# A gated delta rule on raw keys and queries: norms as factors by token and in the output norm's eps

## The chip, the cores and the metric

One core of one Trainium2 chip runs the kernel. The metric is the device time of one launch in microseconds (us), the median of three runs; the kernel before takes 2573.53 us (2573.46 to 2574.1). The engines are TensorE (PE, its weight loads PEld), VectorE (DVE), ScalarE (ACT), GpSimd (POOL) and SyncE (SP), which issues most DMAs.

## The reference, cut to what matters

The reference is a decoder trunk of two layers on 256 tokens of width 2048: a mixer, a cross attention and a convolutional feed-forward net in each layer, all in float32. The change is in the mixer of layer 0, which joins eight stick-breaking attention heads with eight gated delta rule heads of 128 features. For each delta head:

```python
def l2norm(x):
    return x * lax.rsqrt(jnp.sum(x * x, axis=-1, keepdims=True) + EPS)

gq, gk, gv = split(silu(causal_dwconv(gdn_qkv, sconv_w)))
o_b = gated_delta_rule(l2norm(gq), l2norm(gk), gv, log_decay, beta)
o_b = rmsnorm(o_b, gdn_norm) * silu(gdn_gate)
# in gated_delta_rule, by chunks of 64 tokens, q scaled by dk ** -0.5:
neg_n = -where(tri_strict, (k * beta) @ k.T * decay, 0)
t_inv = (1 - neg_n) ** -1                     # by doubling
u = t_inv @ (v * beta);  w = t_inv @ (k * beta * exp(gc))
attn = q @ k.T * decay;  q_g = q * exp(gc);  k_dec = k * exp(gc_last - gc)
# per chunk: v_new = u - w @ state; o = q_g @ state + attn @ v_new
#            state = state * exp(gc_last) + k_dec.T @ v_new
```

So keys and queries each get a norm per token before the rule, and the rule's output gets an RMS norm per token, with EPS = 1e-6 in all of them.

## The kernel before, in words

Activations lie with features on the 128 partitions and the 256 tokens along the free axis. Weights stream from HBM through SP's queue in slabs of 128 x 1024 (`raw`, five buffers). ACT casts each to a high part (`hi`, L250), DVE computes the rest (`lo`, two instructions of 512 columns, L259), and `mm_tile` multiplies them: per step of 128 input features a 512-column matmul on `hi` (L287) and a 256-column one on `lo` (L288). After each such step it calls `side.tick()`.

`Side` holds side chains, written as Python generators. A tick runs at most one step of one chain that is due; `yield n` asks for n ticks until the next step. So the stream of projections on TensorE carries the small work of the heads between its matmuls, in program order as the compiler's scheduler then places it. Three chains at most are open (four from the stick heads on).

The mixer of layer 0 is `even()`. Its order: the first projection while the input arrives; `decays` (from L506), a side chain that makes the per-token factors `g`, `gc`, `bt` (beta), `nbt` (minus beta), `beg` (beta times exp of the summed decay) and `ekd`; then `delta_head` for the eight delta heads, with four projections each (key, query, value, gate: 4 x 16 ticks), in pairs; after each pair a side chain `delta_pair` is spawned. Then come `values` and `stick_head` for the stick-breaking heads, whose chains (`stick_chain`) use `nsu`. The output projection reads the delta heads' results first.

`delta_pair` before, for two heads at once:

- L604 to L607: `squares_of` for the keys and for the queries of both heads: a square (L585, ACT), its float32r part (L586, ACT) and the rest (L587, POOL).
- L608 to L614: `sum_squares`, two 256-column matmuls with a matrix of ones (L593), which gives the sum over the features to every partition; `rsqrt`, a root with one correction (L353 DVE; L355, L356, L358 ACT; L359, L361 DVE) on 256 columns, with single-buffered tiles; and the scaled key or query into `kq` (L613, DVE).
- L616 to L624: `gs`, the summed decays (L621), and `pk`, the products of the keys with keys and queries (L623).
- L625 to L638: the decay factors by `Exp`, then the strict products `p0` (scaled by `nbt`), the attention `at`, and `qg`.
- L640 to L652: transposes of keys and values (L645, L646) and their scaled forms `kbe`, `kd`, `vb` on ACT.
- L655 to L711: p's transpose (L658) and the inverse by doubling (L683, L685, L691, L693); L714 to L753: `u` and `w`, and the four chunks of the state, with the output in PSUM, `po`.
- L755 to L764: the output norm, by `squares_of` and `sum_squares` and one root for each head, the gain (L760), the gate (L761) and the split into two parts (L236, L237).

The PSUM tiles of these steps come from `acc()`, a pool of three buffers. In SBUF the tags `kq0` and `kq` have two buffers each; the stick heads use both tags again.

Of the kernel before, what the change touches and what calls it, by code (L numbers as in the profile page):

```python
# [10 lines left out]
F32 = mybir.dt.float32  # L11
# [3 lines left out]
ALU = mybir.AluOpType  # L15
# [41 lines left out]
CEV = ["B64", "H0", "H1", "U64", "nSU", "nones", "maskT", "mask2", "I64", "maskS"]  # L57
# [90 lines left out]
def build(tc, nc, a):  # L148
# [303 lines left out]
    def even():  # L452
# [12 lines left out]
        for k in range(KD):  # L465
# [7 lines left out]
            if k == 2:  # L473
                wab = [e(f"wab{i}", (P, 512), 2, F32R, "kq0") for i in range(2)]
                A.copy(wab[0], early["ab", 0])
                V.tensor_tensor(out=wab[1], in0=early["ab", 0], in1=f32(wab[0]), op=ALU.subtract)
# [17 lines left out]
        cev = e("cev", (P, 3 * P), tag="sbv")  # L494
        cst = e("cst", (P, 7 * P))
        C = {k: cev[:, q * P:q * P + P] for q, k in enumerate(CEV[:3])}
        C.update({k: cst[:, q * P:q * P + P] for q, k in enumerate(CEV[3:])})
# [8 lines left out]
        def decays():  # L506
            nc.sync.dma_start(cev, a["cev"][:, 0:3 * P])
            nc.sync.dma_start(cst, a["cev"][:, 3 * P:10 * P])
# [20 lines left out]
            V.tensor_scalar(out=g, in0=sl, scalar1=-1.0, scalar2=None, op0=ALU.mult)  # L529
            sigmoid_(bt, ab[:, :, 8:16])  # L530
# [35 lines left out]
        def delta_head(h):  # L566
            kq0 = e("kq0", (P, 2, S), 2)
# [12 lines left out]
        onesr = e("onesr", (P, P), dt=F32R)  # L580

        def squares_of(x):

            sq, sp = tmp("sq", bufs=2), e("sqs", (P, 2, S), 4, F32R, "sqs")
            A.activation(sq, x, AF.Square)  # L585
            A.copy(sp[:, 0], sq)  # L586
            G.tensor_tensor(out=sp[:, 1], in0=sq, in1=f32(sp[:, 0]), op=ALU.subtract)  # L587
            return sp

        def sum_squares(sp):  # L590
            ps = acc()
            for i in range(2):
                T.matmul(ps[:, 0:256], lhsT=onesr, rhs=sp[:, i], start=i == 0, stop=i == 1)  # L593
            return ps

        def delta_pair(h0, kq0s, vs, sgts):

            cc = lambda z, t, i: z[:, t, h0 + i:h0 + i + 1]
            two = range(2)
            if h0 == 0:  # L600
                A.copy(onesr, ones)
            vec = lambda n: e(n, (P, 2, P), 2)
            kq = [e("kq", (P, 2, 2, P), 2) for _ in two]
            sps = []  # L604
            for q in range(2):
                sps.append([squares_of(kq0s[i][:, q]) for i in two])
                yield 6  # L607
            for q in range(2):  # L608
                for i in two:
                    ps = sum_squares(sps[q][i])  # L610
                    r = rsqrt(ps, 256, 1.0).rearrange("p (t n) -> p t n", t=2)
                    z = kq0s[i][:, q].rearrange("p (t n) -> p t n", t=2)
                    V.scalar_tensor_tensor(out=kq[i][:, :, q], in0=z, scalar=P ** -0.5 if q else 1.0, in1=r, op0=ALU.mult, op1=ALU.mult)  # L613
                yield 14 if q else 4  # L614
# [3 lines left out]
            for i in two:  # L618
# [3 lines left out]
                for t in range(2):  # L622
                    T.matmul(pk[:, t * 256:t * 256 + 256], lhsT=kq[i][:, t, 0], rhs=kq[i][:, t].rearrange("p q n -> p (q n)"), start=True, stop=True)  # L623
                pks.append(pk)  # L624
            p0, at, qg = ([vec(n) for _ in two] for n in ("p0", "atf", "qg"))  # L625
            for i in two:
                pk = pks[i].rearrange("p (t c) -> p t c", t=2)
# [6 lines left out]
                A.activation(qg[i].rearrange("p t n -> p (t n)"), gs[:, i * 256:i * 256 + 256], AF.Exp)  # L634
                for t in range(2):
                    V.scalar_tensor_tensor(out=p0[i][:, t], in0=pk[:, t, 0:P], scalar=cc(nbt, t, i), in1=p0[i][:, t], op0=ALU.mult, op1=ALU.mult)
                V.tensor_tensor(out=at[i], in0=pk[:, :, P:2 * P], in1=at[i], op=ALU.mult)
                G.tensor_tensor(out=qg[i], in0=kq[i][:, :, 1], in1=qg[i], op=ALU.mult)  # L638
            yield 5
            kbe, vb = ([vec(n) for _ in two] for n in ("kbe", "vb"))  # L640
            kd = [e("kd", (P, 4, P), 2) for _ in two]
            for i in two:
                px = acc()
                for t in range(2):
                    T.transpose(px[:, t * 256:t * 256 + 128], kq[i][:, t, 0], ident)  # L645
                    T.transpose(px[:, t * 256 + 128:t * 256 + 256], vs[i][:, t * P:t * P + P], ident)  # L646
                for t in range(2):
                    pt = px[:, t * 256:t * 256 + 128]
                    A.activation(kbe[i][:, t], pt, AF.Identity, scale=cc(beg, t, i))
                    for b in range(2):  # L650
                        A.activation(kd[i][:, 2 * t + b], pt, AF.Identity, scale=cc(ekd[:, b], t, i))
                    A.activation(vb[i][:, t], px[:, t * 256 + 128:t * 256 + 256], AF.Identity, scale=cc(bt, t, i))  # L652
# [102 lines left out]
            sps = [squares_of(po[:, i * 256:i * 256 + 256]) for i in two]  # L755
            yield 12
            for i in two:
                pn = sum_squares(sps[i])
                r = rsqrt(pn, 256, 1.0 / P)
                V.scalar_tensor_tensor(out=r, in0=po[:, i * 256:i * 256 + 256], scalar=col("gdn"), in1=r, op0=ALU.mult, op1=ALU.mult)  # L760
# [3 lines left out]
                mix[8 + h0 + i] = x  # L764

# [8 lines left out]
        def stick_chain(h, q, k):  # L774
            if h == 0:
                A.copy(nsu, C["nSU"])
# [669 lines left out]
```

## Time and profile before

| | |
|---|---|
| median of three runs | 2573.53 us (2573.46 to 2574.1) |
| profiled execution | 2573.3 us, span 2571.5 us |
| granted TensorE clock | 0.999 |
| ACT L250, `hi` | 887.8 us busy in 847 instructions |
| DVE L259, `lo` | 1168.0 us busy in 1697 |
| PE L287 on `xs` | 1446.3 us busy in 4112 |
| PE L593, sums of squares | 48 matmuls of 256 columns, median 281 ns |

The span runs from the first to the last instruction; the execution's own time lies 1.8 us above it. A group of the profile has a line of the kernel, an engine, an operation and tile names (output, then inputs), with shapes, a count, the busy time and the mean of one instruction. Matmuls are pipelined: the next starts before the one before it ends, so busy time on PE is not the cost of an instruction; the step from start to start is. Waits are named by what released them last.

### The profile page before, as it was taken

What the parts mean: (1) busy time and instruction counts of PE and PEld (TensorE: products, weight loads), DVE (VectorE), ACT (ScalarE), POOL (GpSimd) and SP (SyncE); (2) the same over time, 40 slices, a digit from 0 to 9 for tenths busy, and PEclk for the clock granted to TensorE, in tenths of its full rate; (3) what the DMA queues carried; (4) which work ended last, traced back from release to release, by engine and by line L of the source; (5) the groups of instructions that cost most, each with busy time, mean ns of one, the idle gap of its engine ahead of it and who ended that gap; (6) DMA issues with size and microseconds to landing.
All of it is one profiled execution on the core that took longest, in us unless ns stands there. A gap on an engine that the chain in (4) does not pass through costs nothing.

```text
span 2571.5 us, 40527 instructions
## 1 busy us (share of the span) xinstructions
PE 2547.2 (99%) x14860; PEld 2215.9 (86%) x14860; DVE 1944.5 (76%) x3968; ACT 1485.5 (58%) x2521; POOL 172.8 (7%) x230
## 2 busy tenths in 40 slices
PE   9999999999999999999999999999999999999998
PEld 7888888888888888888888888888988888888886
DVE  8898776867877767767777677876877767757755
ACT  7677656656655545545456555754755545545544
POOL 2001100302000000000011012120200000000001
PEclk9999999999999999999999999999999999999999
DMA  7333345654555555555555544365555555555554
GB/s 243 129 122 124 124 149 174 211 182 160 194 191 190 191 189 189 190 189 189 194 185 186 190 155 164 132 213 172 181 189 189 191 193 188 189 191 189 191 191 139
DMA packets 127689, 459.06 MB, mean 179 GB/s; under 512 B 14305, under 2 KB 14945, under 8 KB 127361
## 3 DMA queue, kind: packets, MB, share of 16 engines
q1 hardware_dynamic: 126144, 454.63, 53.2%
q8 instruction: 116, 1.90, 0.3%
q10 hardware_dynamic: 1344, 1.84, 0.2%
q14 instruction: 85, 0.69, 0.1%
HBM read 454.32 MB, written 2.10 MB: 177 GB/s over the span
## 4 chain that ended last, share of the span: by engine, by line
PE 92%; DVE 4%; ACT 2%; issue 0%; POOL 0%; DMA 0%; ACTq 0%; POOLq 0%
PE g L287 47%; PE g L288 24%; PE g L1274 3%; PE g L1273 3%; PE g L1272 3%; PE g L336 2%; PE g L339 2%; PE g L337 2%; DVE lo L259 1%; DVE cv L558 1%; PE ps_a L685 1%; DVE xs L241 0%; PE g L298 0%; PE g L297 0%; PE g L299 0%
## 5 line engine op out<-in xcount | busy, mean ns | idle before, releaser
L259 DVE TENSOR_TENSOR lo<-raw,hi 128x512 fp32r<-128x512 f32 (+1 forms) x1697 | 1168.0, 704 | 499.3 <-ACT hi L250 484.5
L287 PE MATMUL g<-xs,hi 128*128 128x512 f32 x4112 | 1446.3, 394 | 1.2 <-DVE xs L241 1.0
L250 ACT CAST hi<-raw 128x1024 fp32r<-128x1024 f32 (+1 forms) x847 | 887.8, 1049 | 813.0 <-PE g L287 436.2
L288 PE MATMUL g<-xs,lo 128*128 128x256 f32 x4112 | 1157.1, 282 | 0.0
L287 PEld LDWEIGHTS g<-xs,hi 128*128 128x128 f32 x4112 | 771.6, 188 | 168.3 <-DVE xs L241 3.4
L288 PEld LDWEIGHTS g<-xs,lo 128*128 128x128 f32 x4112 | 774.1, 188 | 2.7 <-DVE lo L259 0.6
L287 PE MATMUL g<-hid,hi 128*128 128x512 f32 x704 | 244.5, 391 | 0.0
L288 PE MATMUL g<-hid,lo 128*128 128x256 f32 x704 | 197.6, 281 | 0.0
L380 POOL TENSOR_TENSOR sqacc<-sqacc,sq 128x256 f32<-128x256 f32 x115 | 104.7, 915 | 1256.9 <-ACT sq L379 1253.6
L287 PE MATMUL g<-mix,hi 128*128 128x512 f32 x508 | 177.1, 392 | 0.0
L1217 DVE SCALAR_TENSOR_TENSOR fc<-y,cg,fc 128x255 f32<-128x255 f32 x352 | 167.8, 477 | 1.0 <-ACT fc L1215 0.7
L287 PEld LDWEIGHTS g<-hid,hi 128*128 128x128 f32 x704 | 132.1, 188 | 28.8
L288 PE MATMUL g<-mix,lo 128*128 128x256 f32 x508 | 142.9, 281 | 0.0
L1274 PE MATMUL g<-hi,hid 128*128 128x512 f32 x352 | 138.1, 392 | 0.0
L1273 PE MATMUL g<-lo,hid 128*128 128x512 f32 x352 | 138.0, 392 | 0.0
L1272 PE MATMUL g<-hi,hid 128*128 128x512 f32 x352 | 138.0, 392 | 0.0
L288 PEld LDWEIGHTS g<-hid,lo 128*128 128x128 f32 x704 | 132.6, 188 | 0.0
L347 DVE TENSOR_TENSOR y<-g,t 128x256 f32<-128x256 f32 x285 | 118.6, 417 | 4.6 <-ACT t L345 4.0
L287 PEld LDWEIGHTS g<-mix,hi 128*128 128x128 f32 x508 | 95.4, 188 | 20.5
L1215 ACT ACTIVATE fc<-y,cg 128x256 f32<-128x256 f32 x176 | 105.3, 600 | 2.8 <-DVE y L1213 2.8
L345 ACT COPY t<-g 128x256 f32<-128x256 f32 x285 | 103.0, 362 | 6.1 <-PE g L288 5.9
L288 PEld LDWEIGHTS g<-mix,lo 128*128 128x128 f32 x508 | 95.7, 188 | 0.0
(365 smaller groups left out, 2665.0 us busy)
## 6 DMA issues: line engine op xcount, KB each, us to landing
raw<-w SPq DMA_DIRECT2D x845, 512.0 KB, 3.3
raw<-mem SPq DMA_DIRECT2D x8, 512.0 KB, 3.6
X<-x SPq DMA_DIRECT2D x8, 256.0 KB, 5.7
gb<-fin SPq DMA_DIRECT2D x1, 1024.0 KB, 5.4
out<-xg SPq DMA_DIRECT2D x4, 256.0 KB, 2.6
out<-xg ACTq DMA_DIRECT2D x4, 256.0 KB, 2.9
raw<-w SPq DMA_DIRECT2D x2, 384.0 KB, 5.4
cg<-cg SPq DMA_DIRECT2D x1, 591.5 KB, 7.6
```

Of the source, the lines that this page charges most:

```text
L250: A.copy(hi[:, 0:n], raw)
L259: V.tensor_tensor(out=lo[:, s], in0=raw[:, s], in1=f32(hi[:, s]), op=ALU.subtract)
L287: T.matmul(ps[0:m, 0:512], lhsT=hi[:, w], rhs=xs[k], start=first and q == 0, stop=False)
L288: T.matmul(ps[0:m, 0:256], lhsT=lo[:, w], rhs=xs[k][:, 0:256], start=False, stop=last and q == n - 1)
L345: A.copy(t[0:m], ps[0:m, 256:512])
L347: V.tensor_tensor(out=y[0:m], in0=ps[0:m, 0:256], in1=t[0:m], op=ALU.add)
L380: eng.tensor_tensor(out=self.acc[eng], in0=self.acc[eng], in1=q, op=ALU.add)
L1215: A.activation(c, y, AF.Identity, scale=col(f"fc{l}", n * 3 + 2), bias=col(f"fb{l}", n))
L1217: V.scalar_tensor_tensor(out=c[:, s:], in0=y[:, 0:S - s], scalar=col(f"fc{l}", n * 3 + 2 - s), in1=c[:, s:], op0=ALU.mult, op1=ALU.add)
L1272: T.matmul(ps[t], lhsT=xh, rhs=hi[:, w], start=k == 0, stop=False)
L1273: T.matmul(ps[t], lhsT=xh, rhs=lo[:, w], start=False, stop=False)
L1274: T.matmul(ps[t], lhsT=xl, rhs=hi[:, w], start=False, stop=k == FJ - 1)
```

## The change

The keys and queries stay raw (`kq0`); `kq`, `squares_of` and `sum_squares` are gone.

- The raw keys of both heads are transposed first, so that tokens lie on the partitions; ACT copies them to `kt`, and four squares with a row sum (`accum_out`) give each token's sum. One root for the pair's four columns (two heads, two token halves) gives the factor r. It is folded into per-token factors: `nbt` times r squared scales `p0`, `bt` times r scales the values, `beg` times r squared scales the keys of `w`. `kd` takes the raw keys.
- The rule is linear in the query, so its norm goes into the output norm's eps: the raw query's squares, scaled, (`sqq`) are added to the output's squares before they are summed over the features.
- The output norm runs on both heads at once: 512 columns wide, two matmuls of 512, one root; the rest of the float32r split moves from POOL to DVE.
- A list `busy` lets a pair start only when the pair before it has ended. The steps ask for other numbers of ticks.
- `kq0` has four buffers instead of two, and the stick heads' tiles take that tag; `nsu` and `onesr` are filled in `decays`; one constant moves between two tiles.

The core of the diff:

```diff
-            kq0 = e("kq0", (P, 2, S), 2)
+            kq0 = e("kq0", (P, 2, S), 4)
...
-            kq = [e("kq", (P, 2, 2, P), 2) for _ in two]
-            sps = []
-            for q in range(2):
-                sps.append([squares_of(kq0s[i][:, q]) for i in two])
-                yield 6
-            for q in range(2):
-                for i in two:
-                    ps = sum_squares(sps[q][i])
-                    r = rsqrt(ps, 256, 1.0).rearrange("p (t n) -> p t n", t=2)
-                    z = kq0s[i][:, q].rearrange("p (t n) -> p t n", t=2)
-                    V.scalar_tensor_tensor(out=kq[i][:, :, q], in0=z, scalar=P ** -0.5 if q else 1.0, in1=r, op0=ALU.mult, op1=ALU.mult)
-                yield 14 if q else 4
+            while busy:
+                yield 1
+            busy.append(h0)
...
+            px = acc()
+            for i in two:
+                for t in range(2):
+                    T.transpose(px[:, i * 256 + t * P:i * 256 + t * P + P], kq0s[i][:, 0, t * P:t * P + P], ident)
+            kt = e("kt", (P, 4, P))
+            A.copy(kt.rearrange("p c n -> p (c n)"), px)
+            rr = e("rr", (P, 8, 2, 2))
+            for i in two:
+                for t in range(2):
+                    A.activation(tmp("sq", (P, P), 2), kt[:, 2 * i + t], AF.Square, accum_out=rr[:, 0, t, i:i + 1])
+            yield 8
+            V.tensor_scalar(out=rr[:, 1], in0=rr[:, 0], scalar1=1.0, scalar2=EPS, op0=ALU.mult, op1=ALU.add)
+            A.activation(rr[:, 2], rr[:, 1], AF.Ln)
+            A.activation(rr[:, 2], rr[:, 2], AF.Exp, scale=-0.5)
+            A.activation(rr[:, 3], rr[:, 2], AF.Square)
...
-                    T.matmul(pk[:, t * 256:t * 256 + 256], lhsT=kq[i][:, t, 0], rhs=kq[i][:, t].rearrange("p q n -> p (q n)"), start=True, stop=True)
+                    T.matmul(pk[:, t * 256:t * 256 + 256], lhsT=kq0s[i][:, 0, t * P:t * P + P], rhs=kq0s[i][:, :, t * P:t * P + P], start=True, stop=True)
...
+            V.scalar_tensor_tensor(out=rr[:, 3], in0=rr[:, 3], scalar=-0.5, in1=rr[:, 1], op0=ALU.mult, op1=ALU.mult)
+            V.scalar_tensor_tensor(out=rr[:, 3], in0=rr[:, 3], scalar=1.5, in1=rr[:, 2], op0=ALU.add, op1=ALU.mult)
+            V.tensor_tensor(out=rr[:, 4], in0=rr[:, 3], in1=rr[:, 3], op=ALU.mult)
+            for q, z, j in ((5, nbt, 4), (6, bt, 3), (7, beg, 4)):
+                V.tensor_tensor(out=rr[:, q], in0=of(z), in1=rr[:, j], op=ALU.mult)
+            sc = lambda q, t, i: rr[:, q, t, i:i + 1]
+            sqq = e("sqq", (P, 512))
...
-                    V.scalar_tensor_tensor(out=p0[i][:, t], in0=pk[:, t, 0:P], scalar=cc(nbt, t, i), in1=p0[i][:, t], op0=ALU.mult, op1=ALU.mult)
+                    V.scalar_tensor_tensor(out=p0[i][:, t], in0=pk[:, t, 0:P], scalar=sc(5, t, i), in1=p0[i][:, t], op0=ALU.mult, op1=ALU.mult)
...
+                A.activation(sqq[:, i * 256:i * 256 + 256], kq0s[i][:, 1], AF.Square, scale=P * EPS ** 0.5)
             yield 5
...
-            sps = [squares_of(po[:, i * 256:i * 256 + 256]) for i in two]
+            v, y = [z.rearrange("p t q n -> p (t q n)") for z in uws]
+            A.activation(v, po, AF.Square)
+            V.tensor_tensor(out=v, in0=v, in1=sqq, op=ALU.add)
+            sp = e("sqs", (P, 2, 512), dt=F32R)
+            A.copy(sp[:, 0], v)
+            V.tensor_tensor(out=sp[:, 1], in0=v, in1=f32(sp[:, 0]), op=ALU.subtract)
             yield 12
+            pn = acc()
             for i in two:
-                pn = sum_squares(sps[i])
-                r = rsqrt(pn, 256, 1.0 / P)
-                V.scalar_tensor_tensor(out=r, in0=po[:, i * 256:i * 256 + 256], scalar=col("gdn"), in1=r, op0=ALU.mult, op1=ALU.mult)
+                T.matmul(pn, lhsT=onesr, rhs=sp[:, i], start=i == 0, stop=i == 1)
+            V.tensor_scalar(out=v, in0=pn, scalar1=1.0 / P, scalar2=EPS * EPS * P, op0=ALU.mult, op1=ALU.add)
+            A.activation(y, v, AF.Ln)
+            A.activation(y, y, AF.Exp, scale=-0.5)
+            A.activation(sqq, y, AF.Square)
+            yield 8
+            V.scalar_tensor_tensor(out=v, in0=sqq, scalar=-0.5, in1=v, op0=ALU.mult, op1=ALU.mult)
+            V.scalar_tensor_tensor(out=v, in0=v, scalar=1.5, in1=y, op0=ALU.add, op1=ALU.mult)
+            V.scalar_tensor_tensor(out=v, in0=po, scalar=col("gdn"), in1=v, op0=ALU.mult, op1=ALU.mult)
...
+            busy.remove(h0)
...
-            qk = e("sbqk", (P, 2, S), 2, tag="kq")
+            qk = e("sbqk", (P, 2, S), 4, tag="kq0")
```

More of the change, by code (lines that the diff above doesn't have):

```diff
@@ L473, in even @@
             if k == 2:
-                wab = [e(f"wab{i}", (P, 512), 2, F32R, "kq0") for i in range(2)]
+                wab = [e(f"wab{i}", (P, 512), 4, F32R, "kq0") for i in range(2)]
                 A.copy(wab[0], early["ab", 0])
@@ L493, in even @@
         mix, vts = [None] * 16, [None] * 2
[L494 to L497, printed above, removed]
+        cev = e("cev", (P, NEV * P), tag="sbv")
+        cst = e("cst", (P, 6 * P))
+        C = {k: cev[:, q * P:q * P + P] for q, k in enumerate(CEV[:NEV])}
+        C.update({k: cst[:, q * P:q * P + P] for q, k in enumerate(CEV[NEV:])})
+        onesr, nsu = [e(n, (P, P), dt=F32R) for n in ("onesr", "nsu")]
         strict = e("strict", (P, P), dt=I32)
@@ L529, in decays @@
             V.tensor_scalar(out=g, in0=sl, scalar1=-1.0, scalar2=None, op0=ALU.mult)
+            A.copy(nsu, C["nSU"])
+            A.copy(onesr, ones)
             sigmoid_(bt, ab[:, :, 8:16])
@@ L578, in even @@
         halves = (slice(0, 64), slice(64, 128))
[L580 to L594, printed above, removed]
+        busy = []
         def delta_pair(h0, kq0s, vs, sgts):
@@ L641, in delta_pair @@
             kd = [e("kd", (P, 4, P), 2) for _ in two]
+            px = acc()
             for i in two:
[L643 removed]
                 for t in range(2):
[L645 to L646 removed]
+                    T.transpose(px[:, i * 256 + t * P:i * 256 + t * P + P], vs[i][:, t * P:t * P + P], ident)
+            for i in two:
                 for t in range(2):
[L648 to L649 removed]
+                    k = kt[:, 2 * i + t]
+                    A.activation(kbe[i][:, t], k, AF.Identity, scale=sc(7, t, i))
                     for b in range(2):
[L651 to L652 removed]
+                        A.activation(kd[i][:, 2 * t + b], k, AF.Identity, scale=cc(ekd[:, b], t, i))
+                    A.activation(vb[i][:, t], px[:, i * 256 + t * P:i * 256 + t * P + P], AF.Identity, scale=sc(6, t, i))
             yield 6
@@ L770, in stick_head @@
             side.spawn(stick_chain(h, qk[:, 0], qk[:, 1]))
-        nsu = e("nsu", (P, P), dt=F32R)
         def stick_chain(h, q, k):
-            if h == 0:
-                A.copy(nsu, C["nSU"])
             yield 12
@@ L780, in stick_chain @@
             T.matmul(ps[:, 256:384], lhsT=k[:, 128:256], rhs=q[:, 128:256], start=False, stop=True)
-            l = e("sbl", (P, 384), 2, tag="kq0") if h < 4 else mp.tile([P, 384], F32, name="sbl", tag="xs", bufs=16)
+            l = e("sbl", (P, 384), 4, tag="kq0") if h < 4 else mp.tile([P, 384], F32, name="sbl", tag="xs", bufs=16)
             softplus_neg_abs(l, ps[:, 0:384])
```

18 lines of the change are left out of this document (11 added, 7 removed).

## Prediction

> **What bounds the kernel now.** I read four views in this order: the page, a table by stage, the waits of TensorE's queue in the stage that the change touches, and TensorE's timeline around the longest of those waits. The page first (busy us, share of the span, instructions; then the chain that ended last):
>
> ```profile
> span 2571.5 us, 40527 instructions
> PE 2547.2 (99%) x14860; PEld 2215.9 (86%) x14860; DVE 1944.5 (76%) x3968; ACT 1485.5 (58%) x2521; POOL 172.8 (7%) x230
> PE 92%; DVE 4%; ACT 2%; issue 0%; POOL 0%; DMA 0%; ACTq 0%; POOLq 0%
> ```
>
> TensorE is the bound: 99% busy, and 92% of the chain. Whatever the change saves on VectorE, ScalarE or GpSimd counts only where TensorE waits for it. So I ask where TensorE is not busy. The stages (start:end, length, then busy us of PE, PEld, DVE, ACT, POOL):
>
> ```profile
> 36.00:141.00 105.00, 100.95 (x732) 87.37 (x731) 92.84 (x224) 77.01 (x187) 16.58 (x20) 1.00 0.42 138
> 141.00:211.00 70.00, 66.86 (x535) 57.69 (x534) 62.02 (x155) 51.72 (x126) 7.14 (x10) 1.00 0.36 121
> 211.00:281.00 70.00, 66.92 (x524) 57.16 (x523) 61.98 (x156) 51.63 (x126) 7.14 (x10) 1.00 0.36 121
> 281.00:335.00 54.00, 52.54 (x437) 44.67 (x436) 39.03 (x99) 33.16 (x77) 2.10 (x4) 1.00 0.39 128
> 335.00:490.00 155.00, 155.00 (x871) 135.77 (x870) 112.59 (x220) 96.34 (x173) 19.50 (x23) 1.00 0.53 174
> ```
>
> One delta pair takes one period of 70 us. TensorE is idle about 3.1 us in each of the two middle periods, 4.1 in the first stretch, 1.5 in the last, and not at all from 335 on. DVE is 62 of 70 us busy: close behind, but not the bound. The waits of TensorE from 36 to 335 us (total, times, longest) name the idle time, and two waits of its weight loads are for later use:
>
> ```profile
> PE ps_a L593 <- DVE rs_v L353: 5.1, 4, 1.4
> PE ps_a L623 <- DVE kq L613: 2.6, 3, 1.0
> PE ps_a L593 <- ACT sg L443: 2.4, 3, 0.8
> PE ps_a L536 <- DVE gd L529: 1.1, 1, 1.1
> ```
>
> ```profile
> PEld ps_a L683 <- ACT pt L663: 1.3, 4, 0.4
> PEld g L288 <- DVE lo L259: 0.3, 2, 0.2
> ```
>
> Ten of these waits, 10.1 us, stand before two lines: L593, the sum of squares over partitions, and L623, the key products, which read the normalised keys and queries. The projection stream hardly waits for its own weights (0.3 us at L288), so filling the ten gaps is not at once taken back by DVE.
>
> **The ten waits (removed).** What one costs in time is the step from start to start beyond the usual one:
>
> ```profile
> 205.89 0.64 PE L593 MATMUL ps_a<-sqs,onesr 128*128 128x256 f32 x4
> 206.37 0.39 PE L287 MATMUL g<-xs,hi 128*128 128x512 f32 x1
> ...
> 208.73 0.47 PE L593 MATMUL ps_a<-sqs,onesr 128*128 128x256 f32 x2 [0.82 <-ACT sg L443]
> ```
>
> ```profile
> 211.36 0.28 PE L288 MATMUL g<-xs,lo 128*128 128x256 f32 x1
> 211.48 0.39 PE L287 MATMUL g<-xs,hi 128*128 128x512 f32 x1
> 211.71 0.28 PE L288 MATMUL g<-xs,lo 128*128 128x256 f32 x1
> 213.27 0.47 PE L593 MATMUL ps_a<-sqs,onesr 128*128 128x256 f32 x2 [1.28 <-DVE rs_v L353]
> ```
>
> ```profile
> 227.51 0.85 PE L287 MATMUL g<-xs,hi 128*128 128x512 f32 x3
> 229.37 1.13 PE L623 MATMUL ps_a<-kq 128*128 128x256 f32 x4 [1.01 <-DVE kq L613]
> 230.34 0.27 PE L645 MATMUL ps_a<-cg,kq 128*128 128x128 f32 x1
> ```
>
> A 256-column matmul takes 0.28 us but the next starts 0.12 after it; a 512-column one 0.39, the next after 0.23. So each shown wait costs 0.16 us more than its printed idle time (211.71 to 213.27 is 1.56, of which 0.12 is usual). The ten cost 10.1 + 10 x 0.16 = **11.7 us**. All seven at L593 precede query sums: by the program the third and fourth sums of a pair need one of the three PSUM buffers back, which L353, the first step of an earlier root, still has to read (where the row names sg, an input of nothing here, I take the same cause). L623 waits for the last scaled query. The change does away with both reasons: the key norm comes from four transposes and four squares with a row sum, the query norm needs no sum of its own, and L623 reads kq0, which was written many projections earlier.
>
> **The sums themselves (removed).** Per pair eight 256-column matmuls, in four pairs 32. From 205.89 to 206.37 four take 0.48 us, 0.12 each: 32 x 0.12 = **3.8 us** of TensorE. The output's sums stay, in another shape: four of 256 columns (0.48 us) become two of 512 (2 x 0.23): nothing. Eight transposes per pair, 16 passes of L621 and eight of L623 remain; the transposes of the keys only move ahead.
>
> **The other engines.** Means in ns behind the count:
>
> ```profile
> L353 DVE TENSOR_SCALAR rs_v<-ps_a 128x256 f32<-128x256 f32 x22 | 9.1, 416 | 0.0
> L613 DVE SCALAR_TENSOR_TENSOR kq<-kq,rs_q 128x256 f32<-128x256 f32 x16 | 6.6, 415 | 0.0
> L760 DVE SCALAR_TENSOR_TENSOR rs_q<-po,cg,rs_q 128x256 f32<-128x256 f32 x6 | 2.8, 472 | 0.0
> L528 DVE TENSOR_TENSOR sl<-sl,ea 128x16 f32<-128x16 f32 x1 | 0.2, 166 | 0.0
> L529 DVE TENSOR_SCALAR gd<-sl 128x16 f32<-128x16 f32 x1 | 0.7, 705 | 0.0
> L355 ACT ACTIVATE rs_y<-rs_v 128x256 f32<-128x256 f32 x22 | 9.2, 419 | 4.0 <-DVE rs_v L353 4.0
> L586 ACT CAST sqs<-sq 128x256 fp32r<-128x256 f32 x23 | 8.9, 402 | 0.0
> L651 ACT ACTIVATE kd<-ps_a,ekd 128x128 f32<-128x128 f32 x32 | 10.9, 415 | 0.0
> L442 ACT ACTIVATE bt<-bt 128x16 f32<-128x16 f32 x1 | 0.2, 205 | 0.0
> L587 POOL TENSOR_TENSOR sqs<-sq,sqs 128x256 fp32r<-128x256 f32 x22 | 17.9, 824 | 114.8 <-ACT sqs L586 114.8
> L250 ACT CAST hi<-raw 128x1024 fp32r<-128x1024 f32 x72 | 76.2, 1059 | 28.8 <-PE g L287 27.6 <-PE g L339 1.1
> ```
>
> ```profile
> L1277 DVE TENSOR_TENSOR xb<-g,xb 128x512 f32<-128x512 f32 x32 | 21.3, 685 | 13.1 <-PE g L1274 13.1
> L1285 ACT ACTIVATE fq<-xb 128x512 f32<-128x512 f32 x8 | 5.0, 630 | 8.7 <-DVE xb L1277 8.7
> L1158 ACT ACTIVATION_READ_ACCUMULATOR xsc<-ps_a,xmx 128x1 f32 x16 | 3.1, 196 | 0.0
> ```
>
> DVE per pair: four times four steps of 0.416 (three of the root and L613) go, -6.7 us. Seven steps on four columns come; their price lies between 0.17 (L528) and 0.71 (L529, which ran once): 1.2 to 4.9. I take the first, as the plainer row; the choice moves only DVE's load. The output's eight steps of 256 columns (3 x 0.416 + 0.472, twice: 3.4) become six of 512 at 0.69 (4.1). Net about -4.8 of 62. ACT per pair: four squares and four casts at 0.40 and twelve root steps at 0.42 go, -8.2; a copy of 512 columns (0.63), four squares of 128 with a read (0.415 + 0.196 each), three small steps (0.205) and two squares of 256 come, +4.5; the output's ten steps (4.1) become five of 512 at 0.63 (3.2). Net -4.6. POOL loses six subtractions of 0.82. I book nothing for all of this: TensorE's work hides it, and were that cover gone it would be a gain. The two copies into nsu and onesr only move earlier, at under 0.42 us each on ACT.
>
> [...]
>
> **New waits.** Behind the keys' transposes stands a new serial chain before p can be scaled: copy, square, scale, Ln, Exp, Square, two corrections, r squared, the product with nbt, p: 11 hops. Its cover is 8 + 5 + 6 ticks of the projection stream before p's transposes; a tick is 0.35 us (211.36 to 211.71), so 6.65 us. What a hop costs, the old root shows on DVE:
>
> ```profile
> 147.75 0.41 DVE L353 TENSOR_SCALAR rs_v<-ps_a 128x256 f32<-128x256 f32 x1
> ...
> 150.54 0.41 DVE L361 SCALAR_TENSOR_TENSOR rs_q<-rs_q,rs_y 128x256 f32<-128x256 f32 x1
> ```
>
> Six hops in 3.2 us, 0.53 each: 11 x 0.53 = 5.8, just inside the cover. At the output, square, add, cast, subtract (2 x 0.63 + 2 x 0.69 = 2.6 us) stand under 12 ticks (4.2 us). So two places per pair, eight in all, are close. The bounds of one such wait: 0, or the longest seen, 1.4 + 0.16 = 1.56, which makes 12.5 us in eight. Nearest is L683, a chain step of the same kind behind ACT: 1.3 / 4 = 0.33 each; 8 x 0.33 = **2.6 us** is what I take. The gate "busy" holds a pair back until the one before is done: a pair's steps ask for 115 ticks (129 before) and pairs are 128 ticks apart, so it should be passed at once; if not, only the side chain is late, which nobody on TensorE needs until the output projection.
>
> **The sum.** 11.7 + 3.8 - 2.6 = 12.9 us. The profiled execution took 2573.3 us (its span and 1.8 around it): 2560.4. The median of the three runs is 2573.53, 0.2 above, so **2560.6**.
>
> **Rivals.**
> 1. *The waits come back elsewhere.* At both new places TensorE waits as long as it did at worst: 15.5 - 12.5 = 3.0 us gained, 2570.5, no change. For it: the chain fills its cover. Against it: every engine there gets lighter, and the three PSUM buffers are less contended.
> 2. *Slower: the small hops queue behind ScalarE's weight casts.* If each of the 11 hops waits behind one cast (L250, 1.06 us) besides its 0.53, the chain takes 17.5 us, 10.8 beyond its cover; 4 x 10.8 = 43 us, 2573.5 + 43 - 15.5 = 2601. It ends slower than before by over 0.2% from 1.08 us per hop on ((6.65 + 20.6 / 4) / 11). Against it stand the 0.53 of a root that queued behind the same casts.
> 3. *L623 slows down.* Its moving operand, 256 columns in a row, becomes two runs of 128 that lie 256 apart. If such a pattern doubled its pass (229.37 to 230.34 is four, 0.24 each), 32 passes cost 7.7 us: 2568.3, on the edge of no change. No matmul here reads such a pattern, so the trace neither shows nor excludes it. [...]
> 4. *More relief.* With lighter engines no new wait appears and older ones shorten too: 15.5 us, and up to 18.5 with the idle time that is left from 36 to 335 us (11.8 - 10.1 = 1.7) and L683's 1.3: 2555.0 to 2558.
>
> **The numbers.** 0.2% is 5.1 us, about what a measurement of this kernel can tell from no change. Forecast (7 to 15 us gained) 0.69, rival 4 0.12, rival 3 0.05 (half of it faster), rival 1 0.10, rival 2 0.04. Faster 0.69 + 0.12 + 0.03 = 0.84; same 0.12; slower 0.04. The range leaves out rival 2 and most of rival 1: 2554.5 (rival 4, and the 0.6 by which the three runs of before differ) to 2568.5.
>
> **What would show it.** Right: in the table by stage a middle period of about 67 us instead of 70; no line among TensorE's waits for the key products; one root sum of two 512-column matmuls per pair; 32 fewer 256-column ones; DVE some 57 us busy per period. Wrong: waits of over 1 us before the transposes of p, of the values, or before the output's sum; passes of the key products over 0.24 us apart; the projection stream waiting for lo or hi.

## The result, and the profile after

The kernel after takes **2549.89 us** (median of four runs, 2549.8 to 2550.15) against 2573.52 (2573.46 to 2574.1) of the kernel before beside it: a ratio of 0.9908, 95% interval 0.9894 to 0.9922, 23.6 us less. The forecast was 2560.6 with a range down to 2554.5: the direction came true, the size did not; 10.7 us more went than were booked. The profiled execution took 2549.89 us, its span is 2548.1. The page of after (busy us, share, instructions; then the chain):

```profile
span 2548.1 us, 40315 instructions
PE 2532.4 (99%) x14820; PEld 2205.7 (87%) x14820; DVE 1923.3 (75%) x3924; ACT 1467.5 (58%) x2477; POOL 151.3 (6%) x206
PE 94%; DVE 3%; ACT 3%; issue 0%; DMA 0%; POOL 0%; SPq 0%; ACTq 0%; POOLq 0%
```

TensorE is still the bound, and its share of the chain rises from 92% to 94%. The table by stage (as before; the middle periods are now cut at 63 us):

```profile
36.00:141.00 105.00, 103.22 (x774) 90.39 (x772) 93.23 (x244) 81.22 (x209) 9.11 (x12) 1.00 0.43 139
141.00:204.00 63.00, 62.84 (x510) 55.09 (x510) 55.11 (x142) 46.24 (x114) 2.10 (x4) 1.00 0.40 133
204.00:267.00 63.00, 62.82 (x508) 54.35 (x508) 55.23 (x142) 46.25 (x112) 2.10 (x4) 1.00 0.41 134
```

A middle pair is done in 63 us instead of 70, and TensorE is idle for 0.2 us of it instead of 3.1. But 2.9 us of idle time do not make 7 us: TensorE also does the same pair in less busy time. That is the reading that the prediction lacks. Lines have other numbers in after: the doubling's L685 and L693 are L697 and L705, the value transposes L657, p's transposes L670, the key products L624 and the output's sum L776. Of TensorE's waits from 36 to 335 us one is left (engine, tile, line, releaser: us in all, times, longest). Behind it stands the row of the weight loads that answers to L683:

```profile
PE ps_a L657 <- DVE atf L647: 1.6, 1, 1.6
```

```profile
PEld ps_a L695 <- ACT pt L675: 1.6, 5, 0.5
```

The waits at the sums and at the key products are gone, and so is L536's 1.1. One new wait stands ahead of a value transpose (L657, in the first pair alone). TensorE's timeline of after at the sum of the output norm and at the key products (start, us, line, tiles, shape, count):

```profile
65.39 1.03 PE L624 MATMUL ps_a<-kq 128*128 128x256 f32 x4
66.26 0.61 PE L622 MATMUL ps_a<-cst,gd 128*128 128x128 f32 x4
...
246.10 0.63 PE L776 MATMUL ps_a<-sqs,onesr 128*128 128x512 f32 x2
```

One sum of two 512-column matmuls is left per pair, and four passes of L624 take 66.26 - 65.39 = 0.87 us, 0.22 each, not more than before.

To see where 23.6 us went I added up, in both traces, the steps from start to start of TensorE's matmuls over the first 1600 matmuls of the projection stream, which hold the whole delta stage: the 1600th starts at 410.6 us of the span before and at 387.4 after, 23.2 us earlier. "Ahead" is what the last projection step before a group of small matmuls takes beyond its usual 0.23 or 0.12 us.

| part (own + ahead, us) | before | after | difference |
|---|---|---|---|
| sums over partitions | 7.5 + 7.4 | 1.9 + 0.0 | -13.0 |
| key products, summed decays | 9.8 + 3.2 | 9.7 + 0.0 | -3.3 |
| transposes | 4.9 + 0.3 | 4.8 + 2.0 | +1.6 |
| **inverse by doubling** | 28.7 + 4.6 | 24.6 + 2.6 | **-6.2** |
| u, w and the state | 24.2 + 0.0 | 24.1 + 0.1 | 0.0 |
| other small matmuls (L536) | 16.1 + 1.4 | 15.7 + 0.1 | -1.6 |
| between projection matmuls | 9.2 | 8.5 | -0.8 |

The doubling has the same 704 matmuls in both kernels, as the trace counts them: each of the 352 in the program is two instructions there. Its groups, from 0 to 490 us (count, then busy us and mean ns of one, then idle time ahead), in before and in after:

```profile
L685 PE MATMUL ps_a<-st 64*64 64x128 f32 (+1 forms) x320 | 21.6, 260 | 0.3
L693 PE MATMUL ps_a<-st 64*64 64x64 f32 x256 | 13.0, 219 | 0.0
```

```profile
L697 PE MATMUL ps_a<-st 64*64 64x128 f32 (+1 forms) x320 | 17.4, 262 | 0.4
L705 PE MATMUL ps_a<-st 64*64 64x64 f32 x256 | 10.7, 220 | 0.0
```

Counts and means agree, yet the two lines keep TensorE busy 28.1 us instead of 34.6: more of the matmuls run at the same time. The timelines show how. A late step of the doubling in before, then in after:

```profile
246.22 0.45 PE L685 MATMUL ps_a<-st 64*64 64x64 f32 x8
246.50 0.40 PE L693 MATMUL ps_a<-st 64*64 64x64 f32 x8
246.83 0.38 PE L288 MATMUL g<-xs,lo 128*128 128x256 f32 x1
247.05 0.40 PE L287 MATMUL g<-xs,hi 128*128 128x512 f32 x1
247.38 0.45 PE L685 MATMUL ps_a<-st 64*64 64x64 f32 x8
```

```profile
217.53 0.46 PE L697 MATMUL ps_a<-st 64*64 64x64 f32 x16
217.81 0.41 PE L705 MATMUL ps_a<-st 64*64 64x64 f32 x16
218.15 0.50 PE L288 MATMUL g<-xs,hi 128*128 128x512 f32 x1
```

In before, one head's 16 matmuls take 0.61 us (246.22 to 246.83) and the other head's stand in the next place, mixed with eight of the first head's next step: 24 in 0.67 us (247.38 to 248.05). In after, all 32 take 0.62 us (217.53 to 218.15). By the program, the matmuls of one head write the 64 partitions that they read, those of the other head the other 64; in turns, both heads' 32 cost 0.62 us, where one head's 16 cost 0.61.

Not every step of after gets there. It has 14 places with 32 of these matmuls, as many as a step of both heads has; call them two-head steps. In seven of them all 16 of L697 stand ahead of all 16 of L705, with the heads in turns, as the kernel's loops write them (the written order); these cost 0.62 to 0.86 us. In the other seven the lines are mixed, and they cost 1.10 to 1.53. Before has 11 two-head steps, none in the written order, at 1.00 to 1.74 us. TensorE's waits in the doubling are small in both kernels (0.40 us in all before, 0.55 after), so the difference in the doubling's own time is one of order and not of waiting.

### The profile page after: what moved, and what is told of

Same layout as the page of the kernel before. It is cut to its first block, busy times and chain, and to the rows that moved or that the text cites. A ratio compares the mean times of both kernels' runs of the same rounds, so it can differ in the third digit from the quotient of the medians.

```text
span 2548.1 us, 40315 instructions
## 1 busy us (share of the span) xinstructions
PE 2532.4 (99%) x14820; PEld 2205.7 (87%) x14820; DVE 1923.3 (75%) x3924; ACT 1467.5 (58%) x2477; POOL 151.3 (6%) x206
## 4 chain that ended last, share of the span: by engine, by line
PE 94%; DVE 3%; ACT 3%; issue 0%; DMA 0%; POOL 0%; SPq 0%; ACTq 0%; POOLq 0%
PE g L288 48%; PE g L289 25%; PE g L1297 3%; PE g L1296 3%; PE g L1295 3%; PE g L337 2%; PE g L340 2%; PE g L338 2%; DVE lo L260 1%; PE ps_a L697 1%; ACT hi L251 0%; DVE xs L242 0%; DVE cv L562 0%; PE g L299 0%; PE g L298 0%
## 5 line engine op out<-in xcount | busy, mean ns | idle before, releaser
L288 PE MATMUL g<-xs,hi 128*128 128x512 f32 x4112 | 1445.5, 394 | 1.9 <-DVE xs L242 1.6
L288 PEld LDWEIGHTS g<-xs,hi 128*128 128x128 f32 x4112 | 771.6, 188 | 170.3 <-DVE xs L242 4.0
L288 PE MATMUL g<-hid,hi 128*128 128x512 f32 x704 | 244.5, 391 | 0.0
L288 PE MATMUL g<-mix,hi 128*128 128x512 f32 x508 | 177.1, 392 | 0.0
L288 PEld LDWEIGHTS g<-hid,hi 128*128 128x128 f32 x704 | 132.1, 188 | 28.8
L348 DVE TENSOR_TENSOR y<-g,t 128x256 f32<-128x256 f32 x285 | 118.8, 418 | 3.5 <-ACT t L346 3.1
L288 PEld LDWEIGHTS g<-mix,hi 128*128 128x128 f32 x508 | 95.4, 188 | 20.5
```

The costliest lines, as they stand in the source:

```text
L288: T.matmul(ps[0:m, 0:512], lhsT=hi[:, w], rhs=xs[k], start=first and q == 0, stop=False)
L348: V.tensor_tensor(out=y[0:m], in0=ps[0:m, 0:256], in1=t[0:m], op=ALU.add)
```

## The experiments

Two theories for the part of the gain that was not booked. **Theory 1**: the doubling's price depends on where its matmuls stand in program order, both heads in turns, with steps far enough apart that the operands are there. Before, the roots ahead made the chain late, and it caught up in steps a few projection matmuls apart (35 places in program order, one to eight projection matmuls apart within a pair; after has 26, most often twelve apart). **Theory 2**: lighter VectorE, ScalarE and GpSimd. The kernel before took 2573.35 to 2573.62 us beside every experiment, so times can be set side by side.

**Ten more ticks ahead of the key products, in before** (14 becomes 24).

```diff
-                yield 14 if q else 4
+                yield 24 if q else 4
```

> The kernel before with one number changed: 24 ticks instead of 14 between the query sums and the key products, so that the products and the doubling are placed when their inputs are really there. Theory 1 (the changed kernel's unforeseen 6 us in the doubling come from the chain being on time, so that both heads' small matmuls stand together and wait less): the waits at L623 (3.1 us) go and some 3 to 6 us of the doubling: 2564.5 to 2567.5. Theory 2 (they come from lighter VectorE and ScalarE, whose work here is the same as before): only the 3.1 us: about 2570.4, and the doubling's own matmul time stays near 28.7 us.

Measured 2578.26 us (2576.95 to 2579.81), ratio 1.0019 (1.0009 to 1.0029): a miss for both, 4.9 us more. Two stretches at half clock (61.05 and 166.87 us, see the last section) are up to 3.4 of it, by the estimate there. TensorE's waits to 335 us:

```profile
PE g L288 <- DVE lo L259: 3.5, 2, 1.8
PE ps_a L623 <- DVE kq L613: 3.3, 3, 1.4
PE ps_a L593 <- ACT hi L250: 2.5, 3, 0.9
```

The waits moved and did not go: ten ticks more there do not undo them, and the doubling stays at 33.2 us, own and ahead, with none of its 12 two-head steps in the written order.

**Fifteen fewer ticks ahead of the doubling, in after** (8, 5 and 6 become 2, 1 and 1).

```diff
-            yield 8
+            yield 2
...
-            yield 5
+            yield 1
...
-            yield 6
+            yield 1
```

> The changed kernel with 2, 1 and 1 ticks instead of 8, 5 and 6 ahead of the doubling: the same work, but the side chain is placed 15 ticks earlier, before it is ready. Theory 1: waits appear ahead of the transposes of p and in the doubling, 3 to 6 us: 2553 to 2556. Theory 2: nothing changes by over 1 us: 2549 to 2551.

Measured 2553.97 us (2553.84 to 2554.08), ratio 0.9924 (0.9909 to 0.9939): 4.1 more than after, 3.7 of it in the doubling (27.2 to 31.0 us, own and ahead), with the same work: none of its 15 two-head steps stands in the written order, where after has seven. For theory 1.

**The wide output norm alone, in before.**

```diff
-            sps = [squares_of(po[:, i * 256:i * 256 + 256]) for i in two]
+            A.activation(v, po, AF.Square)
...
-                pn = sum_squares(sps[i])
-                r = rsqrt(pn, 256, 1.0 / P)
+                T.matmul(pn, lhsT=onesr, rhs=sp[i], start=i == 0, stop=i == 1)
```

> The kernel before with only the output norm made 512 columns wide (one root for both heads, subtraction on VectorE; the small square and the first correction of that root stay in two halves). The root frees one PSUM buffer earlier, so the first query sum of pairs 2 to 4 should no longer wait (3 x 1.0 us); the other waits at L593 and L623 stay. Theory 1: as the following chain is a little less late, up to 3 us of the doubling as well: 2567 to 2571. Theory 2: VectorE gets 0.7 us more per pair, so only the 3 us: 2570.5 or more.

Measured 2584.2 us (2583.36 to 2585.85), ratio 1.0042 (1.0027 to 1.0057): 10.85 us slower than before beside it, a miss. TensorE's waits:

```profile
PE ps_a L593 <- POOL sqs L587: 6.3, 5, 3.3
PE ps_a L623 <- DVE kq L613: 5.5, 3, 2.5
```

This half of the change, with the narrow squares and roots still beside it, makes the waits longer; and the granted clock falls to 0.95 from 141 to 281 us (below).

**The narrow output norm, in after**: one root of 256 columns for each head, with GpSimd's subtraction.

```diff
-            A.activation(v, po, AF.Square)
-            V.tensor_tensor(out=v, in0=v, in1=sqq, op=ALU.add)
+                A.activation(sq, po[:, c], AF.Square)
+                V.tensor_tensor(out=sq, in0=sq, in1=sqq[:, c], op=ALU.add)
```

> The changed kernel with the output norm by head as before (two roots of 256 columns, four sums of 256, subtraction on GpSimd), the raw queries' squares still added. Both theories: the key and query sums and their waits stay away, so nearly the whole gain stays: 2549.5 to 2552. If the wide output root were what brings the gain: 2560 or more.

Measured 2551.85 us (2551.3 to 2551.87), ratio 0.9915 (0.9901 to 0.993): the change without its wide output norm brings all but 2 us.

**The doubling further apart, in after** (7 ticks instead of 6 behind each step, 10 ahead of it).

```diff
-            yield 6
+            yield 10
...
-                yield 6
+                yield 7
```

> The changed kernel with one number of ticks more per step of the doubling (7 instead of 6) and 10 instead of 6 ahead of it: the same work, more room between one step's matmuls and the next. A pair then asks for 125 ticks of the 128 there are. Theory 1 (what a step of the doubling costs TensorE depends on how long before it the other engines finished the step before, for both heads): the doubling gets cheaper by another 1 to 4 us: 2546 to 2549. Theory 2 (lighter engines): no change, 2549 to 2551.

Measured 2553.26 us (2553.09 to 2553.38), ratio 0.992 (0.9905 to 0.9935). The doubling got 0.6 us cheaper, but the steps of the state 2.6 dearer: a miss for both theories, and no road to a faster kernel.

**The doubling close together, in after** (2 ticks instead of 6).

```diff
-                yield 6
+                yield 2
```

> The changed kernel with 2 ticks instead of 6 per step of the doubling: the same work on every engine, but its steps are placed before the other engines have finished the step before, as in the kernel before. Theory 1: the doubling costs TensorE 4 to 7 us more: 2554 to 2557. Theory 2: 2549 to 2551.

Measured 2557.68 us (2557.53 to 2557.89), ratio 0.9938 (0.9921 to 0.9954): 7.8 us more by the distance alone, a little above the forecast of theory 1. The doubling's groups to 490 us:

```profile
L697 PE MATMUL ps_a<-st 64*64 64x128 f32 (+1 forms) x320 | 21.9, 261 | 0.7
L705 PE MATMUL ps_a<-st 64*64 64x64 f32 x256 | 13.8, 222 | 0.0
```

That is the price of before (34.6 us busy) and a little more, with the same work on every engine as after. None of its 14 two-head steps stands in the written order any more (1.11 to 1.53 us each), while the waits in the doubling are only 0.2 us longer than in after.

**The doubling further apart, in before** (9 ticks instead of 6).

```diff
-                yield 6
+                yield 9
```

> The kernel before with one number changed: nine ticks instead of six behind each step of the inverse by doubling. All the work, all roots and sums stay as they were. In program order the doubling's matmuls now stand at 26 places instead of 35, those of both heads together, 9 to 18 projection steps apart. Theory 1 (what TensorE pays for the doubling depends on where it stands: both heads together and the operands long ready): the doubling and the step ahead of it fall from 33.4 us to about 28, so 2567 to 2569. Theory 2 (the doubling became cheaper because VectorE, ScalarE and GpSimd have less to do): nothing changes in that load, so 2573.5, or up to 2 us more as the chain is longer.

Measured 2572.19 us (2571.32 to 2572.35), ratio 0.9994 (0.9985 to 1.0003): no change in all, where theory 1 said 2567 to 2569: the time is a miss, but the doubling itself did as theory 1 said. The groups:

```profile
L685 PE MATMUL ps_a<-st 64*64 64x128 f32 (+1 forms) x320 | 17.4, 261 | 0.6 <-ACT st L703 0.4
L693 PE MATMUL ps_a<-st 64*64 64x64 f32 x256 | 10.9, 220 | 0.0
```

Nearly the price of after, in before: own and ahead 33.4 became 28.8 us, and five of 12 two-head steps now stand in the written order instead of none. What ate it: the transposes cost 7.7 us more (waits for `qg` and `vb`) and 3 us went between projection matmuls, where the clock fell (0.95 from 141 to 211 us); the sums' waits got 6.8 cheaper.

**Dead work, first try.** Per pair, in every pair: twelve products on VectorE, eleven squares on ScalarE, twelve small products on GpSimd whose results nobody reads.

```diff
+            load_(4, 4, 4)
```

> The changed kernel with about the load put back that it took from the other engines: per pair 12 products of 256 columns on VectorE (0.42 us each), 11 squares of 256 on ScalarE and 12 products of 96 on GpSimd, whose results nobody reads, ahead of the chain's own work in its first three steps. Theory 1: the chain still has its ticks, so the time stays within 2 us: 2549.5 to 2552. Theory 2: the unforeseen 6 us of the doubling come back, and waits with them: 2555 to 2560.

Measured 2571.31 us (2570.87 to 2573.26), ratio 0.9992 (0.9983 to 1.0002). And, in the later three pairs only and without GpSimd:

```diff
+            if h0:
+                load_(4, 4)
```

> The kernel after with dead work in the second, third and fourth pair only, so that the start of the launch is left alone: twelve products of 256 columns on VectorE (5.0 us) and eleven squares of 256 columns on ScalarE (4.6 us) per pair, whose results nobody reads, about the load that the change took off these two; nothing on GpSimd. Theory 1: the doubling keeps its places nearly; 2550 to 2552. Theory 2: the six us of the doubling come back in three of four pairs, 2554.5. By the steady periods of the run with dead load from the first pair on, 1.2 us per pair, it is 2553.5.

Measured 2557.27 us (2557.08 to 2557.36), ratio 0.9937 (0.9924 to 0.9949): above every number expected. Neither tells what it was made for. The dead products of VectorE had no input from their pair, and the compiler placed them early: the second run's 36 ran between 28.9 and 118.8 us. Each made one long wait there (9.3 us at L288 behind ScalarE's cast; 2.4 us ahead of p's transposes), and the clock fell to a half with it, for 13.65 us (8.9 of them idle) and 3.41 us.

**Dead sums in a PSUM buffer of their own, in after**: eight 256-column matmuls per pair ahead of the value transposes; then one of 64 columns. Nobody reads them.

```diff
+            pz = acc()
+            for z in range(8):
+                T.matmul(pz[:, 0:256], lhsT=onesr, rhs=xs[z][:, 0:256], start=z == 0, stop=z == 7)
```

> The changed kernel with eight dead 256-column matmuls per pair, as many as the sums that it removed, on operands that are long ready, in one of the three PSUM buffers. Both theories: the bare price of the removed sums, 32 x 0.12 = 3.8 us: 2553.7; more only if the PSUM buffer is missed elsewhere (up to 2 us).

Measured 2551.84 us (2551.69 to 2552.02), ratio 0.9915 (0.99 to 0.9929): 2.0 more, where 3.8 was expected. The sums cost 3.9 us, and the doubling became 2.3 cheaper: 12 of its 16 two-head steps stand in the written order. The small one:

```diff
+            pz = acc()
+            T.matmul(pz[:, 0:64], lhsT=onesr, rhs=xs[0][:, 0:64], start=True, stop=True)
```

> The kernel after with one dead matmul of 64 columns per pair ahead of the value transposes, in a PSUM buffer of its own from the pool of three; nobody reads it. It turns the order of the three buffers by one for all later steps of the pair. In the run with eight dead sums in such a buffer the doubling was 2.5 us cheaper. If the turned buffers did that, the time is 2549.9 - 2.5 + 0.3 = 2547.7; if the eight sums did it by giving ScalarE and VectorE time, 2550.0 to 2550.3.

Measured 2551.55 us (2551.17 to 2551.72), ratio 0.9914 (0.9901 to 0.9928): 1.7 more, a miss; the doubling became only 0.8 cheaper, so turned buffers are at most a third of what the eight sums did. Most of the 1.7 is the clock (below).

**More ticks ahead of the value transposes, in after** (8 instead of 5).

```diff
-            yield 5
+            yield 8
```

> The kernel after with 8 ticks instead of 5 ahead of the value transposes. The one wait of 1.6 us before the transposes in the first pair should go, 1.6 us for 2548.3. But in program order the doubling now stands at 30 places instead of 26, as the heads are parted in two steps of each pair; by theory 1 that costs 0.2 to 0.6 us at each of the four added places, so 2549 to 2551 in all. Theory 2 has nothing against 2548.3.

Measured 2551.06 us (2550.87 to 2551.14), ratio 0.9912 (0.9899 to 0.9926): the wait of 1.6 us stayed, and the doubling cost 0.6 more at its 30 places. In their own time the steps even became 1.4 cheaper (12 of 14 in the written order), but what stands ahead of them 2.0 dearer, so the order is not the whole price. No version faster than after was found.

**Dead work tied to its pair.** The dead instructions now read tiles of the pair (`kt`, `pt`, `uw`), so they cannot run before it. First VectorE and ScalarE:

```diff
+            for _ in range(nv):
+                V.tensor_tensor(out=dead, in0=src, in1=cst[:, 256:512], op=ALU.mult)
+            for _ in range(na):
+                A.activation(tmp("sq", bufs=2), src, AF.Square)
...
+            load_(kt[:, 0:2].rearrange("p c n -> p (c n)"), 4, 4, 5)
```

> The kernel after with dead work in every pair whose results nobody reads: per pair twelve products of 256 columns on VectorE (5.0 us) and eleven squares of 256 columns on ScalarE (4.6 us), about what the change took off these two. Unlike in the two earlier runs with dead work, each reads a tile of its pair (the transposed keys, p's transpose, u and w), so that it cannot run before the pair does. Theory 1 (the order in which the doubling stands in the program decides, the load does not): in program order the doubling now stands at 33 places instead of 26 and in the two middle pairs in bunches of single heads, so by the rows of the runs with 30 to 35 places some 3 to 5 us of the doubling come back, 2553 to 2555. Theory 2 (the load itself): doubling, re-entry and older waits come back in full, 8.5 us and more, 2558.5 to 2562.

> Only the eleven squares on ScalarE of the placed load. Theory 1: 30 places, 1 to 3 us of the doubling, 2551 to 2553. Theory 2: ScalarE is in the inverse's chain (it copies each step) and in the weights' casts, so it should bring more than half of what both engines bring.

> Only the twelve products on VectorE of the placed load. Theory 1: 27 places, 0 to 1 us, 2550 to 2551. Theory 2: VectorE is the busiest engine beside TensorE (55 of 63 us), so 5 us more on it should bring as much as ScalarE's, 2554 or more.

Measured: both 2553.7 us (2553.45 to 2554.07), ratio 0.9923 (0.9908 to 0.9938); ScalarE's alone 2551.77 (2551.69 to 2552.06), 0.9916 (0.9901 to 0.9931); VectorE's alone 2550.23 (2550.04 to 2550.49), 0.9909 (0.9893 to 0.9926). All three times lie where theory 1 had them. Theory 2 fails with both and with VectorE's alone; ScalarE's alone brought 1.9 of the 3.8 us, about the half at which theory 2 drew its line, and does not part the two. 5 us more per pair on the busiest side engine cost 0.3 us where the doubling nearly kept its places (27). Of the 3.8 us that came with both, 2.6 lie in the doubling at 33 places, and its waits are no longer than in after (0.3 us against 0.55): this part of the load works by the order, as the compiler sets the matmuls down elsewhere. It is not so everywhere: with ScalarE's alone nine two-head steps stand in the written order, more than in after, and yet the doubling costs 1.6 more, with 1.2 us of waits inside it instead of 0.4.

Then with GpSimd, by fifteen and by nine products of 96 columns per pair, and nine on GpSimd alone:

```diff
+            for _ in range(ng):
+                G.tensor_tensor(out=deadg, in0=src[:, 0:96], in1=cst[:, 256:352], op=ALU.mult)
...
-            load_(kt[:, 0:2].rearrange("p c n -> p (c n)"), 4, 4, 5)
+            load_(kt[:, 0:2].rearrange("p c n -> p (c n)"), 4, 4, 3)
```

> The run before it with fifteen dead products of 96 columns per pair on GpSimd besides (about 5 us, what the change took off GpSimd); the order of TensorE's matmuls is the same as there. If GpSimd's load slows VectorE's small steps, as the one step that took 0.70 us in the trace of before, it is 1 to 4 us above that run; if GpSimd lies beside everything, the same within 0.5 us.

> The kernel after with the placed dead work on VectorE and ScalarE and only nine dead products on GpSimd per pair instead of fifteen. From 36 to 335 us the fifteen had raised GpSimd's busy time by 37.8 us (51.69 against 13.94), twice what the change took off it (32.96 to 13.94, 19.0); nine should raise it by some 20. GpSimd's part was 4.6 us with fifteen; in proportion it is 2.5 here, so 2556.2 (2555.5 to 2557). That would be 6.3 us of load, and the rest of the change without it.

> Only the nine dead products on GpSimd per pair, with no dead work on VectorE and ScalarE. TensorE's matmuls stand in program order at the same 26 places as after. If GpSimd slows VectorE's steps by itself, 2 to 3 us here too, 2552 to 2553; if it counts only where VectorE is full already, 2550 to 2550.5.

Measured: fifteen 2558.28 us (2557.9 to 2558.9), ratio 0.9941 (0.9926 to 0.9956), 4.6 above the run without GpSimd's and more than expected; nine 2554.97 (2554.62 to 2555.21), 0.9928 (0.9915 to 0.994), a little below its expectation; GpSimd's nine alone 2550.98 (2550.41 to 2551.11), 0.9912 (0.9898 to 0.9925), between its two. With fifteen and with nine TensorE's matmuls stand in the same order as without them, so GpSimd's part of the load (4.6 and 1.3 us) does not come by the order. The page of the run with nine and the other two engines:

```profile
PE 2537.7 (99%) x14820; PEld 2208.5 (87%) x14820; DVE 1944.0 (76%) x3972; ACT 1480.1 (58%) x2521; POOL 176.0 (7%) x242
```

Its three side engines are nearly as busy as in before (1944.5, 1485.5, 172.8), and it is 5.1 us slower than after. So with the load at these places the lighter engines are worth **5.1 of the 23.6 us**; with it put back, 18.7 us below the kernel before are still there (2573.62 beside this run).

## Why the prediction was right and wrong

- *Bound, waits, sums: right.* Seven waits at L593 and 32 matmuls were priced at 7.5 + 7 x 0.16 + 3.8 = 12.4 us; the sums fell by 13.0. The three at L623 were priced at 3.1; the key products fell by 3.3. (A pair has eight passes of L621, 32 in four pairs, not 16; no term uses them.)
- *New waits: right in kind, 1.0 too dear.* 2.6 us were taken, 1.6 came, ahead of the value transposes and in the first pair alone. A wait of over 1 us there was named as a sign of being wrong; it came once, where eight waits of 0.33 us were booked. The output's sum waits for nothing. The gate `busy` never holds: without it the program comes out the same, instruction for instruction. In the second pair the keys' transposes start at 190.26 us and p's at 201.63: the chain had 11.4 us, as the key products and other small work lie between the same ticks, not the 6.65 that I counted in projection steps alone.
- *The step that failed: "I book nothing for all of this".* The working held that TensorE's own work hides the rest of the pair, so that its price is fixed and lighter engines count only in waits; of the new numbers of ticks it asks only whether they cover the new chain. The price is not fixed. The doubling, 704 matmuls that the change does not touch, cost 6.2 us less, since its matmuls stand in another order; the distance alone moves that price up by 6.9 us, own and ahead, in after (27.2 to 34.1), and down by 4.5 in before (33.4 to 28.8). Some 3.0 us of it came back with the side engines' load, 2.6 of them with VectorE's and ScalarE's, by the order. L536 and the projection stream gave 2.4 more. Together 8.6, and 1.8 from the terms that were booked: 10.4 of the 10.7.
- *DVE some 57 us per period:* 55.2 in 63 us. For the four-column steps the lower price, 0.17 us, was the right one; the group of one of them in after, from 141 to 267 us:

```profile
L612 DVE TENSOR_SCALAR rr<-rr 128x4 f32<-128x4 f32 x2 | 0.3, 163 | 0.0
```

- *Rivals.* 1 and 2 are refuted: no wait of the new chain but one. 3 is refuted: two runs of 128 columns cost what 256 in a row did (0.22 and 0.24 us). 4, "more relief", was nearest with 15.5 to 18.5 us, but it counted idle time alone; the rest was in busy time.
- *Why L536's wait went.* VectorE's and GpSimd's timelines of before, and VectorE's of after:

```profile
58.52 0.70 DVE L529 TENSOR_SCALAR gd<-sl 128x16 f32<-128x16 f32 x1
```

```profile
58.32 0.87 POOL L587 TENSOR_TENSOR sqs<-sq,sqs 128x256 fp32r<-128x256 f32 x1 [6.45 <-ACT sqs L586]
```

```profile
57.21 0.16 DVE L531 TENSOR_SCALAR gd<-sl 128x16 f32<-128x16 f32 x1
```

The step ended within 0.03 us of GpSimd's subtraction (59.22 and 59.19). With no GpSimd work beside it the step takes 0.16 us. The same shows in the run with GpSimd's nine products alone, where L612's step (now L624) takes 366 ns instead of 163. Its group, and then one of GpSimd's dead products with the step that started under it:

```profile
L624 DVE TENSOR_SCALAR rr<-rr 128x4 f32<-128x4 f32 x2 | 0.7, 366 | 0.0
```

```profile
193.96 1.52 POOL L595 TENSOR_TENSOR deadg<-kt,cst 128x96 f32<-128x96 f32 x1
195.14 0.37 DVE L624 TENSOR_SCALAR rr<-rr 128x4 f32<-128x4 f32 x1
```

In the three runs with GpSimd's dead products this step started eleven times while one of them ran, and ended 0.02 to 0.03 us behind it every time; the one time that it started between two of them it took 0.157 us. So in these traces the small step of VectorE that started under an instruction of GpSimd lasted until that was done. The 0.54 us that this cost L529 are about half of L536's wait of 1.1 us; the other half is not traced.

The odd row of 0.70 us was a clue that I had in hand and used only as the upper end of a price.

What stays open: how the half of the doubling's gain that is not load divides between the roots that no longer make the chain late and the other numbers of ticks; and why the first pair's wait at L657 did not move with three more ticks.

## What to carry to other kernels

Small work that rides between a bound engine's main instructions has no fixed price (here the same 704 matmuls cost 27.2 us six ticks apart and 34.1 two ticks apart): compare its busy time and its steps from start to start in the whole stage, not only the waits, and look up in the trace what an edit does to the order in which the compiler sets it down. The 64x64 matmuls of two heads cost half here when they came in turns (32 in 0.62 us, one head's 16 in 0.61); with six ticks between the steps none of before's two-head steps stood so, with nine five of 12. To put a load back as a test, tie it to data of its place, or it runs somewhere else (here 36 products meant for the later three pairs ran between 28.9 and 118.8 us); and half of a change that lightens a chain may be slower than none (here by 10.85 us).

## What the runs showed of the hardware

In some runs the granted clock was 0.50 for stretches of 3.41 us that followed waits of TensorE, and what a wait cost depended on how it fell into these stretches. The run with one dead matmul and after have the same wait (1.59 and 1.58 us), here cut into stretches of the clock's records (PE's busy time is the first number behind the length, the clock the third from the end):

```profile
71.13:74.54 3.41, 1.50 (x11) 1.09 (x10) 3.23 (x11) 3.41 (x12) 1.27 (x2) 1.00 0.01 2
74.54:77.95 3.41, 3.41 (x15) 3.02 (x14) 3.17 (x8) 3.21 (x8) 0.18 (x1) 0.50 0.14 24
```

```profile
69.14:72.55 3.41, 2.64 (x15) 2.04 (x14) 3.19 (x16) 3.41 (x13) 0.73 (x1) 1.00 0.14 56
72.55:75.96 3.41, 2.60 (x18) 2.35 (x19) 3.27 (x10) 3.41 (x12) 0.74 (x1) 1.00 0.01 2
```

Where 1.9 us idle lie in one stretch (waits of 1.59 and 0.32), the next runs at a clock of 0.50. There the four transposes of p and the twelve projection matmuls behind them take 4.22 us, in after 2.88: 1.34 of the 1.66 us between the two kernels. Half of a stretch, 1.7 us, is my estimate of the most that it can lose, from the 3.41 us at 0.50. Where the wait is cut in two (0.8 and 0.8), the clock stays at 1.00. The wide output norm in before had five such stretches, up to 8.5 of its 10.85 us; nine ticks in before had three stretches' length, up to 5.1 us, about what the doubling gave. The limit itself is not settled. Stretches with 1.85 to 2.74 us idle were followed by one at half clock in five runs (one dead matmul, ten more ticks, nine ticks in before, the wide output norm, the smaller dead load). But in the run with ten more ticks one with a single wait of 1.14 us was too (half clock from 61.06 us on), and with nine ticks one of 0.95 us idle that ran at half clock itself. Stretches with 1.36 us idle in before (280.18 to 283.59) and 1.5 in after (2536.98 to 2540.40) were followed by one at 1.00. In the runs with the doubling close together and with more ticks ahead of the value transposes the wait of 1.6 us at L657 came at a mean clock of 1.00 (0 to 300 and 36 to 141 us).
